# Spreading the context branch over sixteen experts: order edges on TensorE, a deferred expert half, four split buffers

## The chip, the cores and the metric

The kernel runs on one core of one Trainium2 chip. The metric is device microseconds of one execution, as the median of the runs shown. TensorE (PE) multiplies matrices, VectorE (DVE), ScalarE (ACT) and GpSimd (POOL) work on tiles, SyncE (SP) only issues transfers. POOL issues transfers too, from its own queue. The five run in parallel, each through its own list of instructions in order, and wait for one another by semaphores.

## The reference

Two blocks of two layers each over 256 tokens x of width 1024, with a context of 256 tokens beside them in each block; all in float32.

```python
def first_block(x, c, ctx, ...):
    for l in range(2):
        # modulation: mod = silu(c) @ w_ada[l] + b_ada[l]: shifts, scales and gates
        # mLSTM mixer over x, its states started from the context
        x = x + gt1 * (mix_x @ w_out[l])
        # 16 experts, each takes its 32 best tokens
        x = x + gt2 * expert_choice_ffn(modulated_rmsnorm(x, ...), w_router[l], w_e_gate[l], w_e_up[l], w_e_down[l])
    return _rms(x, g_final)

def expert_choice_ffn(xn, w_router, w_gate, w_up, w_down):
    aff = softmax(xn @ w_router); gate, idx = top_k(aff.T, 32); xs = xn[idx]
    hid = silu(einsum('ecd,edf->ecf', xs, w_gate)) * einsum('ecd,edf->ecf', xs, w_up)
    return zeros.at[idx].add(einsum('ecf,efd->ecd', hid, w_down) * gate)

def second_block(x, c, ctx, ...):
    # layer 0: Hyena mixer, of x AND of the second context ctx_2; layer 1: attention of x over both
    ...

def hyena_mixer(h, ...):
    proj = h @ w_in                      # 1024 -> 4 x 2048: x0, x1, v, z
    x0, x1, v = split(short_conv(proj[:, :6144]))
    u = x1 * v
    y = irfft(rfft(u, 512) * rfft(k, 512))[:256] + u * d      # k from a small network
    return (y * x0 * silu(z)) @ w_out
```

The second block's context depends on nothing of the first block. So its Hyena layer can run while the first block's last experts do.

## The kernel before

The program is written with a tile framework: pools hand out buffers by tag (with a number of buffers each), and a scheduler sets each engine's order when the program is built, from the order of the code, a simulated time line and the buffers; at run time that order is fixed.

The stretch that the change touches, in order of time:

- **Layer 1's mLSTM mixer** (`mixer`). A part of the modulation (`ada`: loads of `w_ada` or `ada_w_2`, tag `W`, and matmuls of line 191 into `pad`) is stepped through beside other work. `PLACES` says which part goes where: "M1" and "L1" are in the mixer, ahead of and in the mLSTM core, "R1" is in the router. Parts a1, b0, b1 (second block, 16 loads of one MiB) stand in R1. Behind the core comes the output projection of x (lines 109 to 111 with `mhi`, `mlo`), with four loads of `w_out`.
- **The router** (`route_tokens`): norm, logits, top-k, gathering of the tokens into XS.
- **Layer 1's experts** (`experts`, `expert_k`), only for x (`ns == 1`). An expert has 24 steps of line 823: eight each for gate, up (both on XS) and down (on the transposed hidden tile `hT`). A step is four matmuls of 256 columns, side by side on four column groups; the trace has two records for each float32 matmul. Two steps share a weight tile of one MiB. Six first tiles have buffers of their own (`W2`), all others the ring `W` of five, filled from SP's queue.
- **The context's Hyena layer** (`hyena` with `G == 1`), written behind the experts in the code but placed between them by the scheduler. It has 16 pieces of 128 channels (`ct`). A piece has four projections (`projT`: in two halves; each half splits 128x512 weights into a high part `hi`, line 104 on ACT, and a rest `lo`, line 105 on DVE, two buffers each, and issues 12 matmuls, lines 109 to 111 on `hyx`), then `uf` (line 1058 on POOL), its transposes (line 1059), a forward transform with `fe` (line 1017), the product with the filter `Kt`, and the transform back with `fi` (line 1017, four matmuls of 256 columns). Four pieces form a block, which ends in an output projection (`out_proj`, `projN_steps`: steps of six 512-column matmuls on `hmh`, `hml`). Its weights go through a ring `Wb` of two on POOL's queue. Piece 15 is kept back for the last expert: its loads stand on SP's queue behind a gate on expert 14's hidden tile (`self.late[14]`).
- **The end**: `between` makes the second block's input from x, and the latent Hyena layer begins.

Of the kernel before, what the change touches and what calls it, by code (L numbers as in the profile page):

```python
# [13 lines left out]
OP = mybir.AluOpType  # L14
# [7 lines left out]


SB = 4
SA = 3
AB = dict(atp=2, aP=2, aq=3, atk=2)
HB = dict(Yf=1, Y=1, ht1=1)
PLACES = dict(P0="", M0="01 02 10", L0="", R0="a0", W1="", P1="11", M1="12", L1="", R1="a1 b0 b1")
EVERY = dict(P0=3, L0=1, P1=3, L1=1)


class K:
    def __init__(self, ctx, tc, A, out):
# [12 lines left out]
        self.sbufs = 2  # L46
        self.filler = None
        self.side, self.turn = (None, 1), 0
        self.wgate, self.late = [], {}

    def T(self, shape, tag, bufs=1, dt=F32):
# [55 lines left out]
    def mm3(self, out, l, r, start, stop):  # L107
        mm = self.nc.tensor.matmul
        mm(out, lhsT=l[0], rhs=r[0], start=start, stop=False)  # L109
        mm(out, lhsT=l[0], rhs=r[1], start=False, stop=False)  # L110
        mm(out, lhsT=l[1], rhs=r[0], start=False, stop=stop)  # L111

    def rsqrt(self, out, in_, scale):
# [184 lines left out]
    def projN_steps(self, wts, x, tts, n, pss, start=True, stop=True):  # L298
        nk = x[0].shape[1]
        for k in range(nk):  # L300
            hi = self.T([128, n], "hi", self.sbufs, F32R)
            lo = self.T([128, n], "lo", self.sbufs, F32R)
            self.split(wts(k), hi, lo)
            for q, tt in enumerate(tts):
                c = slice(tt * 128, tt * 128 + 128)
                self.mm3(pss[q], (x[0][:, k, c], x[1][:, k, c]), (hi, lo), start and k == 0, stop and k == nk - 1)
            self.fill()
            yield
# [510 lines left out]
    def expert_k(self, ps, w, k, l, M, N, ns):  # L819

        wt = self.ew(w, k, self.nc.sync.dma_start, ns)
        for j, v in enumerate(l):
            self.nc.tensor.matmul(ps[M * j:M * j + M], lhsT=v, rhs=wt[:, j * N:(j + 1) * N], start=(k == 0), stop=(k == 7))  # L823

    def experts(self, l, xs, F2, XS, SgT, R, early, beside=None):
        nc, A, T = self.nc, self.A, self.T
# [8 lines left out]
        nS = N // 128  # L835
        Y = {}
        for e in range(16):
            q, r = divmod(e, 4)
            pgu = []
# [14 lines left out]
            nc.vector.tensor_tensor(hv, hv, pgu[1], op=OP.mult)  # L854
            pt = self.PT([128, nS, 128])
            for i in range(nS):
                nc.tensor.transpose(pt[:, i], hv[:, i * 128:(i + 1) * 128], self.ident)
            hT = T([128, 4, 128], "hT", 2)
            self.copy(hT[:, :nS], pt)
            py = self.P([128, N])  # L860
            for k in range(8):
                j, i = divmod(k, nS)
                self.expert_k(py, A["w_e_down"][l, e], k, [hT[:, i, M * j:M * j + M]] * G, M, N, ns)
            if r == 0:
                Y = {s: T([128, 1024], "Y", ns) for s, _ in xs}
            for i, (s, x) in enumerate(xs):
                for jj in range(G):
                    p0, c = M * jj + 32 * i, slice(jj * N, (jj + 1) * N)
                    nc.vector.tensor_tensor(Y[s][32 * r:32 * r + 32, c], py[p0:p0 + 32], gt[s][p0:p0 + 32, c], op=OP.mult)  # L869
            if r == 3:  # L870
                for s, x in xs:
                    for t in range(2):
                        for n in range(2):
                            ps = self.PS([128, 512])
                            nc.tensor.matmul(ps, lhsT=SgT[s][:, q, t * 128:(t + 1) * 128], rhs=Y[s][:, n * 512:(n + 1) * 512],  # L875
                                             start=True, stop=True)
                            xv = x[:, t, n * 512:(n + 1) * 512]
                            nc.vector.tensor_tensor(xv, xv, ps, op=OP.add)

        if beside is not None:  # L880
# [102 lines left out]
    def hy_consts(self, three):  # L983
# [9 lines left out]
        dma(fi, A["fi"].rearrange("p (k n) -> p k n", k=4))  # L993
        self.fds, self.fis = (fe,), (fi,)
# [26 lines left out]
    def hyena(self, x, X, gt, dma, blocks, G, three, gate=None):  # L1021
# [3 lines left out]
        for g0, wg in blocks:  # L1025
            m = self.parts([128, blocks[0][1], 256], "hm", 1, True)
            for g in range(g0 // G, (g0 + wg) // G):
# [4 lines left out]
                u = self.parts([128, 2, n], "u", 2, three)  # L1032
                x0s = T([128, G, 256], "x0s", G)
                for i in range(G):
                    ct = G * g + i
                    cv = {}
                    for q, kind in enumerate((1, 2, 0, 3)):
# [7 lines left out]
                        if kind < 3:  # L1045
# [6 lines left out]
                            if kind == 2:  # L1052
                                nc.vector.tensor_tensor(cv[1], cv[1], cv[2], op=OP.mult)

                                pt = self.PT([128, 2, 128])
                                uf = T([128, 2, 128], "uf", 2)
                                for c, op in enumerate((OP.add, OP.subtract)):
                                    nc.gpsimd.tensor_tensor(uf[:, c], cv[1][:, :128], cv[1][:, 128:][:, ::-1], op=op)
                                    nc.tensor.transpose(pt[:, c], uf[:, c], self.ident)
                                self.put([v[:, :, i * 128:(i + 1) * 128] for v in u], pt)  # L1060
                        else:
                            sg = T([128, 256], "cvz", G)
                            nc.scalar.activation(sg, ps, AF.Silu)
                            nc.vector.tensor_tensor(x0s[:, i], sg, cv[0], op=OP.mult)
                pu = []
                pu2 = self.PS([128, 2, 2, n]) if G == 1 else None
                for c in range(2):
# [3 lines left out]
                    pu.append(ps)  # L1071
                Yf = T([128, 2, 2, n], "Yf", HB["Yf"] if three else 1)
                t1 = T([128, 2, n], "ht1", HB["ht1"] if three else 1)
# [8 lines left out]
                py = self.PT([128, G, 256])  # L1082
                for i in range(G):
                    for q in range(4):
                        c, f = divmod(q, 2)
                        self.mmx(py[:, i], [v[:, c, f, i * 128:(i + 1) * 128] for v in Y], [v[:, q] for v in self.fis], q == 0, q == 3)
                i0 = G * g - g0
                nc.vector.tensor_tensor(x0s, x0s, py, op=OP.mult)
                self.split(x0s, m[0][:, i0:i0 + G], m[1][:, i0:i0 + G])
            self.out_proj(x, A["hy_w_out_2"][0], m, g0, wg, gt, dma, wg - G if three and g0 + wg == 16 else 0)  # L1090

# [240 lines left out]
    def run(self):  # L1332
# [7 lines left out]
        if True:  # L1340
# [47 lines left out]
            if True:  # L1388
                with self.psum("ps1", mm=2, tp=1, sm=1):
# [3 lines left out]
                    with self.psum("ps2", "right", mm=2, tp=1, sm=1), self.pool("bga"):  # L1393
                        self.wtag, self.wbufs = "Wb", 2
                        c2 = self.load_x("ctx_2", "hc")
                        self.hy_consts(False)
                        a0 = self.modA(b0[1], 1, self.colv["ng", 0], "a1")
                        gtc = self.row_bcast(b0[0][:, 0], 0, 64, 1, "gtc", 1)
                        X2 = self.modulated(c2, a0, b0[1][:, 0], 1)
                        with self.pool("bgb") as p:  # L1400
                            self.route = dict(self.route, rtmp=p)
                            self.rbufs = 1
                            self.hyena(c2, X2, gtc, pool, [(0, 4), (4, 4), (8, 4), (12, 3)], 1, False)
                            keep, ps2 = (self.cur, self.route), self.ps
# [4 lines left out]
                            X = (T([128, 8, 256], "hyl0", 1, F32R), T([128, 8, 256], "hyl1", 1, F32R))  # L1409
                            self.between(x, X, b0)  # L1410
                            (self.cur, self.route), self.ps = keep, ps2
                            self.hyena(c2, X2, gtc, sync, [(15, 1)], 1, False, self.late[14])
# [189 lines left out]
```

## Time and profile before

| | us |
|---|---|
| median of 3 runs | 2360.59 (2359.33 to 2368.23) |
| the profiled execution | 2366.99 |
| its span | 2365.2 |

| share of the span | |
|---|---|
| TensorE busy | 90% |
| DVE / ACT / POOL busy | 53% / 31% / 8% |
| chain that ended last: PE / DVE / issue / DMA / ACT | 72% / 9% / 8% / 7% / 3% |

The page's averages mix stages with different limits, so the table by stage is the view to read first: busy time of each engine in a stretch, the granted TensorE clock (1.00 is 2.4 GHz, 0.50 is 1.2 GHz), the mean busy share of the core's 16 DMA engines (a stretch that is full reads 1.01 or 1.02), and GB/s. Matmuls are pipelined: a later one starts before an earlier one ends, so the time that one takes up is read from start to start.

### The profile page before, as it was taken

The numbers are of one execution on the slowest core, as the hardware profiler recorded it, in microseconds if no ns is written. First come the engines' busy times: TensorE is split into PE (matmuls) and PEld (weight loads), VectorE is DVE, ScalarE is ACT, GpSimd is POOL, SyncE is SP. The second block draws the span as 40 slices with busy tenths as digits, with TensorE's granted clock in tenths as the row PEclk, the third lists the DMA queues.
The fourth block names the chain that finished last, engine by engine and source line by source line (L and its number), as shares of the span: only waits on it lengthen the run. The fifth ranks groups of instructions, "written<-read, shape, count | busy, mean of one in ns | idle before, by whom it ended". The sixth has DMA issues, their size and how long they took to land.

```text
span 2365.2 us, 35049 instructions
## 1 busy us (share of the span) xinstructions
PE 2135.7 (90%) x13966; PEld 1436.1 (61%) x13966; DVE 1250.4 (53%) x2533; ACT 737.5 (31%) x1414; POOL 187.7 (8%) x315
## 2 busy tenths in 40 slices
PE   5999988999999989998799998898777999999998
PEld 3776664343343436864376766665234999979786
DVE  3954444333433337654355555544125878875776
ACT  3323331000000014343233222222013555555665
POOL 1000000011010100000011011100001110100100
PEclk8999999999999999999899999998777999999999
DMA  8247545999999996459799999988996545435320
GB/s 342 99 157 312 204 184 193 413 415 415 414 413 415 414 405 251 137 194 370 295 351 365 372 374 370 351 336 327 421 421 262 185 144 188 168 132 189 126 81 26
DMA packets 129588, 664.09 MB, mean 281 GB/s; under 512 B 12666, under 2 KB 23429, under 8 KB 62352
## 3 DMA queue, kind: packets, MB, share of 16 engines
q1 hardware_dynamic: 115616, 602.89, 66.0%
q0 software_dynamic: 13808, 58.96, 6.6%
q8 instruction: 110, 1.80, 0.3%
q14 instruction: 54, 0.44, 0.1%
HBM read 656.56 MB, written 5.24 MB: 280 GB/s over the span
## 4 chain that ended last, share of the span: by engine, by line
PE 72%; DVE 9%; issue 8%; DMA 7%; ACT 3%; POOL 1%; SPq 0%; DVEq 0%; POOLq 0%; ACTq 0%
PE pmm L823 16%; PE pmm L109 12%; PE pmm L111 11%; PE pmm L110 11%; PE pad L191 3%; PE psm L875 2%; DMA W<-in_w_e_gate 1%; DVE lo L105 1%; DMA W<-in_w_e_up 1%; PE ptp L1017 1%; DMA W<-in_w_ada 1%; PE pmm L798 1%; PE pad L978 1%; DMA W<-in_ada_w 1%; PE ppo L1247 1%
## 5 line engine op out<-in xcount | busy, mean ns | idle before, releaser
L823 PE MATMUL pmm<-W,XS 128*32 128x256 f32 (+1 forms) x3040 | 378.8, 478 | 39.7 <-DMA W<-in_w_e_gate 20.3
L105 DVE TENSOR_TENSOR lo<-W,hi 128x512 fp32r<-128x512 f32 (+1 forms) x420 | 283.7, 680 | 187.1 <-ACT hi L104 184.2
L104 ACT CAST hi<-W 128x512 fp32r<-128x512 f32 (+1 forms) x420 | 255.5, 612 | 352.0 <-PE pmm L110 162.9
L823 PEld LDWEIGHTS pmm<-W,XS 128*32 128x32 f32 (+1 forms) x3040 | 127.0, 123 | 241.3 <-issue 151.1
L823 PE MATMUL pmm<-W,hT 128*32 128x256 f32 (+1 forms) x1536 | 190.1, 483 | 20.2 <-DVE hT L101 8.3
L111 PE MATMUL pmm<-hyx,lo 128*128 128x256 f32 x640 | 191.6, 299 | 10.6 <-DVE lo L105 10.6
L109 PE MATMUL pmm<-hyx,hi 128*128 128x256 f32 x640 | 193.4, 302 | 4.8 <-ACT hi L104 4.8
L110 PE MATMUL pmm<-hyx,hi 128*128 128x256 f32 x640 | 185.8, 290 | 0.0
L105 DVE TENSOR_TENSOR lo<-Wb,hi 128x512 fp32r<-128x512 f32 x160 | 109.4, 692 | 117.3 <-ACT hi L104 116.3
L104 ACT CAST hi<-Wb 128x512 fp32r<-128x512 f32 x160 | 96.8, 619 | 209.4 <-PE pmm L110 138.3
L869 DVE TENSOR_TENSOR Y<-pmm,gt 32x512 f32<-32x512 f32 (+1 forms) x128 | 70.9, 554 | 143.5 <-PE pmm L823 141.8
L109 PE MATMUL pmm<-hyl,hi 128*128 128x256 f32 x512 | 144.5, 283 | 1.7 <-DVE rtmp L697 1.7
L110 PE MATMUL pmm<-hyl,hi 128*128 128x256 f32 x512 | 144.1, 282 | 0.0
L111 PE MATMUL pmm<-hyl,lo 128*128 128x256 f32 x512 | 143.1, 283 | 0.0
L109 PEld LDWEIGHTS pmm<-hyx,hi 128*128 128x128 f32 x640 | 126.6, 198 | 23.7 <-ACT hi L104 16.6
L111 PEld LDWEIGHTS pmm<-hyx,lo 128*128 128x128 f32 x640 | 126.3, 197 | 22.3 <-DVE lo L105 14.1
L823 PEld LDWEIGHTS pmm<-W,hT 128*32 128x32 f32 (+1 forms) x1536 | 65.6, 125 | 117.6 <-issue 68.6
L110 PEld LDWEIGHTS pmm<-hyx,hi 128*128 128x128 f32 x640 | 126.6, 198 | 2.4 <-issue 2.2
L851 ACT ACTIVATE h<-pmm 128x256 f32<-128x256 f32 (+1 forms) x31 | 15.1, 488 | 362.1 <-PE pmm L823 361.9
L191 PE MATMUL pad<-W,cpad 128*32 128x512 f32 x576 | 91.0, 643 | 21.6 <-DMA W<-in_w_ada 16.7
L854 DVE TENSOR_TENSOR h<-h,pmm 128x512 f32<-128x512 f32 (+1 forms) x32 | 17.7, 552 | 171.9 <-ACT h L851 89.5
L109 PEld LDWEIGHTS pmm<-hyl,hi 128*128 128x128 f32 x512 | 97.4, 190 | 3.4 <-issue 1.9
(516 smaller groups left out, 4084.1 us busy)
## 6 DMA issues: line engine op xcount, KB each, us to landing
W<-in_w_e_gate SPq DMA_DIRECT2D x128, 1024.0 KB, 11.2
W<-in_w_e_up SPq DMA_DIRECT2D x128, 1024.0 KB, 11.2
W<-in_w_e_down SPq DMA_DIRECT2D x128, 1024.0 KB, 11.2
W<-in_w_ada SPq DMA_DIRECT2D x48, 1024.0 KB, 6.6
W<-in_hyw SPq DMA_DIRECT2D x32, 1024.0 KB, 5.1
Wb<-in_hyw POOLq DMA_DIRECT2D x30, 1024.0 KB, 8.9
W<-in_ada_w SPq DMA_DIRECT2D x24, 1024.0 KB, 5.2
W<-in_at_w_in SPq DMA_DIRECT2D x16, 1024.0 KB, 5.0
```

The source lines that it names most:

```text
L104: self.nc.scalar.copy(hi, w)
L105: self.nc.vector.tensor_tensor(lo, w, hi.bitcast(F32), op=OP.subtract)
L109: mm(out, lhsT=l[0], rhs=r[0], start=start, stop=False)
L110: mm(out, lhsT=l[0], rhs=r[1], start=False, stop=False)
L111: mm(out, lhsT=l[1], rhs=r[0], start=False, stop=stop)
L191: nc.tensor.matmul(ps[32 * j:32 * j + 32, :], lhsT=self.cpad[:, blk, k0 + k, :], rhs=wt[:, k, j * 512:(j + 1) * 512], start=(k0 + k == 0), ...
L798: nc.tensor.matmul(ps, lhsT=v, rhs=S[s][:, t], start=(t == 0 and q == 0), stop=(t == 1 and q == 1))
L823: self.nc.tensor.matmul(ps[M * j:M * j + M], lhsT=v, rhs=wt[:, j * N:(j + 1) * N], start=(k == 0), stop=(k == 7))
L869: nc.vector.tensor_tensor(Y[s][32 * r:32 * r + 32, c], py[p0:p0 + 32], gt[s][p0:p0 + 32, c], op=OP.mult)
L875: nc.tensor.matmul(ps, lhsT=SgT[s][:, q, t * 128:(t + 1) * 128], rhs=Y[s][:, n * 512:(n + 1) * 512], start=True, stop=True)
L978: nc.tensor.matmul(ps[:, i, f], lhsT=self.fd[:, t, i * 256 + f * 128:i * 256 + (f + 1) * 128], rhs=ab[:, i, t], start=(t == 0), stop=(t == 1))
L1017: self.nc.tensor.matmul(out, lhsT=l[0], rhs=r[0], start=start, stop=stop)
```

## The change

1. **Order edges.** `mm3` returns its first matmul. While `mixed` is set (the first 15 pieces of the context layer), every step of `projT` and `projN_steps` calls `place`: step j may not stand on TensorE's list ahead of the pair of expert steps number 1.2 j - 4. The edge orders only; no semaphore comes of it.
2. **Deferred halves.** In layer 1 an expert's second half (transposes, down, Y) is issued behind the gate and up of the next one. In the context layer, `pend` keeps the back transform and the output projection until `uf` of the next piece has been issued, and the transposes of `uf` are issued one projection later than before.
3. **Four split buffers** `hi` and `lo` for the context layer in place of two (`sbufs`), and two of `Yf`.
4. **Folded back transform.** `fi` is loaded with half its columns; four matmuls of 128 columns give an even and an odd part, and a copy, an addition and a subtraction (reversed) give the two halves. The forward transform was folded already.
5. **PLACES.** Parts a1, b0, b1 of the modulation move from R1 to L1.

Two things stay as they are for x's own Hyena layer (`three`): `flush` is called at once, and its transforms are not folded.

```diff
+SHARE, LEAD = 1.2, 4
-PLACES = dict(P0="", M0="01 02 10", L0="", R0="a0", W1="", P1="11", M1="12", L1="", R1="a1 b0 b1")
+PLACES = dict(P0="", M0="01 02 10", L0="", R0="a0", W1="", P1="11", M1="12", L1="a1 b0 b1", R1="")
...
+    def place(self, first):
+
+        if self.mixed is None:
+            return
+        i = int(self.mixed * SHARE) - LEAD
+        self.mixed += 1
+        if 0 <= i < len(self.clusters):
+            self.tc.add_manual_dep(first.ins, self.clusters[i].ins.name,
+                                   mybir.DependencyInfo(mybir.DependencyClass.NoSync, mybir.DependencyReason.DATA),
+                                   reason="share")
...
-                self.mm3(ps, (hi[:, k], lo[:, k]), (x[0][:, kk, c0:c0 + n], x[1][:, kk, c0:c0 + n]), kk == 0, kk == 7)
+                first = self.mm3(ps, (hi[:, k], lo[:, k]), (x[0][:, kk, c0:c0 + n], x[1][:, kk, c0:c0 + n]), kk == 0, kk == 7)
+                if k == 0:
+                    self.place(first)
...
-            self.nc.tensor.matmul(ps[M * j:M * j + M], lhsT=v, rhs=wt[:, j * N:(j + 1) * N], start=(k == 0), stop=(k == 7))
+            last = self.nc.tensor.matmul(ps[M * j:M * j + M], lhsT=v, rhs=wt[:, j * N:(j + 1) * N], start=(k == 0), stop=(k == 7))
+        if ns == 1 and k % 2:
+            self.clusters.append(last)
...
+            if put_off and e:
+                down(e - 1, last)
+            last = hv
+            if not put_off:
+                down(e, hv)
+        if put_off:
+            down(15, last)
...
-            fe, fi = T([128, 2, 256], "fe"), T([128, 4, 256], "fi")
+            fe, fi = T([128, 2, 256], "fe"), T([128, 4, 128], "fi")
...
-                                    nc.tensor.transpose(pt[:, c], uf[:, c], self.ident)
-                                self.put([v[:, :, i * 128:(i + 1) * 128] for v in u], pt)
+                                if not three:
+                                    self.flush()
...
+                        if q == (1 if three else 2):
+                            pt = self.PT([128, 2, 128])
+                            for c in range(2):
+                                nc.tensor.transpose(pt[:, c], uf[:, c], self.ident)
+                            self.put([v[:, :, i * 128:(i + 1) * 128] for v in u], pt)
...
+                self.pend.append(lambda Y=Y, x0s=x0s, m=m, i0=G * g - g0: self.back(Y, x0s, m, i0, blocks[0][1]))
+                if three:
+                    self.flush()
+            self.pend.append(lambda m=m, g0=g0, wg=wg: self.out_proj(x, A["hy_w_out_2"][0], m, g0, wg, gt, dma,
+                                                                     wg - G if three and g0 + wg == 16 else 0))
+            if three:
+                self.flush()
+        self.flush()
+
+    def flush(self):
+
+        p, self.pend = self.pend, []
+        for f in p:
+            f()
+
+    def back(self, Y, x0s, m, i0, width):
+
+        G = x0s.shape[1]
+        if not m:
+            m += self.parts([128, width, 256], "hm", 1, True)
+        py = self.PT([128, G, 256])
+        if len(Y) == 1:
+
+            for c in range(2):
+                for f in range(2):
+                    self.mmx(py[:, 0, c * 128:(c + 1) * 128], [v[:, c, f] for v in Y], [v[:, 2 * c + f] for v in self.fis],
+                             f == 0, f == 1)
+            y = self.T([128, 2, 128], "yh", 1)
+            ye = self.T([128, 128], "ye", 1)
+            nc = self.nc
+            nc.scalar.copy(ye, py[:, 0, :128])
+            nc.vector.tensor_tensor(y[:, 0], ye, py[:, 0, 128:], op=OP.add)
+            nc.vector.tensor_tensor(y[:, 1], ye[:, ::-1], py[:, 0, 128:][:, ::-1], op=OP.subtract)
+            y = y.rearrange("p a b -> p (a b)")[:, None]
...
+                        self.sbufs = 4
...
+                            self.mixed = 0
                             self.hyena(c2, X2, gtc, pool, [(0, 4), (4, 4), (8, 4), (12, 3)], 1, False)
+                            self.mixed = None
```

How this moves the instructions, at three places. In the names, a letter tag stands before the arrow for the tile written and behind it for those read; lines of the changed program are some 15 to 70 further down (823 becomes 842, 109 becomes 112, 186 becomes 201, 320 becomes 339, 895 becomes 926).

First, TensorE where the context's first fifteen pieces are done, before: expert 11, alone.

```order
L823 MATMUL pmm<-W,XS_7295 32x256 x8
L823 MATMUL pmm<-W,XS_7296 32x256 x16
L823 MATMUL pmm<-W,XS_7295 32x256 x16
L823 MATMUL pmm<-W,XS_7296 32x256 x16
L857 MATMUL ptp<-cf,h_8983 128x128 x2
L823 MATMUL pmm<-W,hT 32x256 x32
L875 MATMUL psm<-Y,SgT 128x512
```

Now, TensorE at the end of gate and up of expert 14 and the start of the down half of expert 13 behind it.

```order
L842 MATMUL pmm<-W,XS_7295 32x256 x8
L842 MATMUL pmm<-W,XS_7296 32x256 x8
L112 MATMUL pmm<-hi,hmh 128x512
L113 MATMUL pmm<-lo,hmh 128x512
L114 MATMUL pmm<-hi,hml 128x512
L842 MATMUL pmm<-W,XS_7296 32x256 x8
L112 MATMUL pmm<-hi,hmh 128x512
L113 MATMUL pmm<-lo,hmh 128x512
L114 MATMUL pmm<-hi,hml 128x512
L864 MATMUL ptp<-cf,h_9348 128x128 x2
L842 MATMUL pmm<-W,hT 32x256 x8
```

Context steps (here of the output projection of pieces 12 to 14) now stand between the pairs of expert steps until expert 14, where before experts 11 to 14 had none between them.

Second, SP's queue ahead of layer 1's experts, before: the modulation's `ada_w` behind the mixer's `w_out`.

```order
L186 DMA W<-in_w_ada 128x2048 x8
L320 DMA W<-in_w_out 128x4x512 x4
L186 DMA W<-in_ada_w 128x2x1024 x4
L186 DMA W<-in_ada_w 128x2048 x8
L186 DMA W<-in_ada_w 128x2x1024 x4
L895 DMA W<-in_w_e_up 128x2048
```

Now, the same place.

```order
L201 DMA W<-in_w_ada 128x2048 x8
L201 DMA W<-in_ada_w 128x2x1024 x4
L201 DMA W<-in_ada_w 128x2048 x8
L201 DMA W<-in_ada_w 128x2x1024 x4
L339 DMA W<-in_w_out 128x4x512 x4
L926 DMA W<-in_w_e_up 128x2048 x2
```

The sixteen loads of a1, b0 and b1 have moved ahead of the four of the output projection.

Third, POOL's queue in the context layer, before.

```order
L1042 DMA Wb<-in_hyw 128x2048
L1058 TENSOR_TENSOR uf<-cv_9720 128x128 x2
L1042 DMA Wb<-in_hyw 128x2048
L1030 DMA Kt<-Kd 128x512
L1042 DMA Wb<-in_hyw 128x2048
L1058 TENSOR_TENSOR uf<-cv_9904 128x128 x2
```

Now, the same place.

```order
L1073 DMA Wb<-in_hyw 128x2048 x2
L1088 TENSOR_TENSOR uf<-cv_9718 128x128 x2
L1061 DMA Kt<-Kd 128x512
L1073 DMA Wb<-in_hyw 128x2048 x2
L1088 TENSOR_TENSOR uf<-cv_9894 128x128 x2
```

Each `uf` now stands behind both weight loads of the next piece, where it stood behind one.

## Rows read from the trace of the kernel before

**Rows 1.** The page's head: span and number of instructions.

```profile
span 2365.2 us, 35049 instructions
```

**Rows 2.** Table by stage: busy us (xcount) of PE, PEld, DVE, ACT, POOL, clock, DMA share, GB/s.

```profile
1020.00:1049.00 29.00, 25.89 (x173) 21.23 (x172) 18.85 (x73) 16.06 (x51) 0.48 (x2) 1.00 0.32 118
1049.00:1101.00 52.00, 50.44 (x236) 27.07 (x236) 21.13 (x41) 15.00 (x28) 2.82 (x4) 0.93 0.77 282
...
1190.00:1640.00 450.00, 411.06 (x3694) 305.71 (x3693) 240.47 (x477) 130.04 (x251) 45.36 (x79) 0.97 0.92 355
1640.00:1756.00 116.00, 78.04 (x808) 29.55 (x806) 14.78 (x30) 2.28 (x6) 0.30 (x2) 0.75 1.00 412
...
1148.00:1786.00 638.00, 543.04 (x4986) 369.86 (x4982) 280.97 (x557) 151.38 (x294) 51.25 (x91) 0.91 0.94 371
...
1330.00:1470.00 140.00, 128.32 (x1205) 96.53 (x1204) 75.61 (x152) 42.35 (x82) 15.64 (x27) 1.00 0.96 373
```

**Rows 3.** TensorE's waits from 1190 to 1640: total us, times, longest; ten rows.

```profile
PE pmm L111 <- DVE lo L105: 10.6, 11, 1.7
PE ptp L1059 <- POOL uf L1058: 7.1, 9, 1.4
...
PE pmm L109 <- ACT hi L104: 4.6, 7, 1.5
...
PE pmm L823 <- DVE hT L101: 1.0, 2, 0.5
```

**Rows 4.** TensorE's groups from 1190 to 1640: count, busy us, mean ns, idle before.

```profile
L111 PE MATMUL pmm<-hyx,lo 128*128 128x256 f32 x475 | 142.8, 301 | 10.6 <-DVE lo L105 10.6
...
L823 PE MATMUL pmm<-W,XS 128*32 128x256 f32 x1152 | 75.9, 385 | 0.0
L823 PE MATMUL pmm<-W,hT 128*32 128x256 f32 x640 | 41.2, 384 | 3.1 <-ACT hT L99 2.1 <-DVE hT L101 1.0
...
L109 PE MATMUL pmm<-hi,hmh 128*128 128x512 f32 x58 | 21.3, 444 | 1.9 <-ACT hi L104 1.9
...
L1059 PE MATMUL ptp<-cf,uf 128*128 128x128 f32 x30 | 9.1, 308 | 7.7 <-POOL uf L1058 7.1
```

**Rows 5.** TensorE in order of time, around 1320: start, us, engine, line, operation.

```profile
1316.66 1.07 PE L823 MATMUL pmm<-W,XS 128*32 128x256 f32 x16
...
1317.88 0.28 PE L109 MATMUL pmm<-hyx,hi 128*128 128x256 f32 x1
1318.00 0.28 PE L110 MATMUL pmm<-hyx,hi 128*128 128x256 f32 x1
...
1323.20 1.05 PE L1017 MATMUL psm<-u,fe 128*128 128x128 f32 x8
...
1326.05 1.99 PE L1017 MATMUL ptp<-fi,Yf 128*128 128x256 f32 x8
1327.69 0.47 PE L109 MATMUL pmm<-hyx,hi 128*128 128x256 f32 x1
```

**Rows 6.** The first layer's experts, layer 1's experts alone, and there TensorE's longest wait.

```profile
440.00:860.00 420.00, 392.98 (x1932) 162.18 (x1930) 139.78 (x235) 17.15 (x29) 40.82 (x76) 1.00 1.01 414
...
1700.00:1750.00 50.00, 32.18 (x324) 11.61 (x324) 2.95 (x7) 1.14 (x3) 0.30 (x2) 0.70 1.01 421
...
PE pmm L823 <- DMA W<-in_w_e_up: 15.1, 14, 2.8
```

**Rows 7.** SP's queue and TensorE in order of time, and line 191 alone by stretch.

```profile
1013.18 6.03 SPq L320 DMA_DIRECT2D W<-in_w_out  x4
1044.47 54.33 SPq L186 DMA_DIRECT2D W<-in_ada_w  x16
...
1049.32 2.51 PE L191 MATMUL pad<-W,cpad 128*32 128x512 f32 x8 [2.68 <-DMA W<-in_ada_w]
1052.91 0.79 PE L109 MATMUL pmm<-hi,mhi 128*128 128x512 f32 x1 [0.46 <-ACT mhi L635]
...
1049.00:1101.00 52.00, 16.76 (x96) 2.77 (x96) 0.93 0.77 282
```

More of the change, by code (lines that the diff above doesn't have):

```diff
@@ L48, in __init__ @@
         self.side, self.turn = (None, 1), 0
+        self.mixed, self.clusters = None, []
         self.wgate, self.late = [], {}
+        self.pend = []
     def T(self, shape, tag, bufs=1, dt=F32):
@@ L108, in mm3 @@
         mm = self.nc.tensor.matmul
-        mm(out, lhsT=l[0], rhs=r[0], start=start, stop=False)
+        first = mm(out, lhsT=l[0], rhs=r[0], start=start, stop=False)
         mm(out, lhsT=l[0], rhs=r[1], start=False, stop=False)
         mm(out, lhsT=l[1], rhs=r[0], start=False, stop=stop)
+        return first
+    def place(self, first):
[7 more added lines that the diff above has]
+                                   reason="share")
     def rsqrt(self, out, in_, scale):
@@ L305, in projN_steps @@
                 c = slice(tt * 128, tt * 128 + 128)
-                self.mm3(pss[q], (x[0][:, k, c], x[1][:, k, c]), (hi, lo), start and k == 0, stop and k == nk - 1)
+                first = self.mm3(pss[q], (x[0][:, k, c], x[1][:, k, c]), (hi, lo), start and k == 0, stop and k == nk - 1)
+                if q == 0:
+                    self.place(first)
             self.fill()
@@ L836, in experts, with down @@
         Y = {}
+        put_off = ns == 1
+        def down(e, hv):
+            q, r = divmod(e, 4)
+            pt = self.PT([128, nS, 128])
+            for i in range(nS):
+                nc.tensor.transpose(pt[:, i], hv[:, i * 128:(i + 1) * 128], self.ident)
+            hT = T([128, 4, 128], "hT", 2)
+            self.copy(hT[:, :nS], pt)
+            py = self.P([128, N])
+            for k in range(8):
+                j, i = divmod(k, nS)
+                self.expert_k(py, A["w_e_down"][l, e], k, [hT[:, i, M * j:M * j + M]] * G, M, N, ns)
+            if r == 0:
+                Y.update({s: T([128, 1024], "Y", ns) for s, _ in xs})
+            for i, (s, x) in enumerate(xs):
+                for jj in range(G):
+                    p0, c = M * jj + 32 * i, slice(jj * N, (jj + 1) * N)
+                    nc.vector.tensor_tensor(Y[s][32 * r:32 * r + 32, c], py[p0:p0 + 32], gt[s][p0:p0 + 32, c], op=OP.mult)
+            if r == 3:
+                for s, x in xs:
+                    for t in range(2):
+                        for n in range(2):
+                            ps = self.PS([128, 512])
+                            nc.tensor.matmul(ps, lhsT=SgT[s][:, q, t * 128:(t + 1) * 128], rhs=Y[s][:, n * 512:(n + 1) * 512],
+                                             start=True, stop=True)
+                            xv = x[:, t, n * 512:(n + 1) * 512]
+                            nc.vector.tensor_tensor(xv, xv, ps, op=OP.add)
         for e in range(16):
-            q, r = divmod(e, 4)
             pgu = []
@@ L854, in experts @@
             nc.vector.tensor_tensor(hv, hv, pgu[1], op=OP.mult)
[L855 to L878, printed above, removed]
+            if put_off and e:
[5 more added lines that the diff above has]
+            down(15, last)
         if beside is not None:
@@ L1025, in hyena @@
         for g0, wg in blocks:
-            m = self.parts([128, blocks[0][1], 256], "hm", 1, True)
+            m = []
             for g in range(g0 // G, (g0 + wg) // G):
@@ L1032, in hyena @@
                 u = self.parts([128, 2, n], "u", 2, three)
-                x0s = T([128, G, 256], "x0s", G)
+                x0s = T([128, G, 256], "x0s", 2)
                 for i in range(G):
@@ L1071, in hyena @@
                     pu.append(ps)
-                Yf = T([128, 2, 2, n], "Yf", HB["Yf"] if three else 1)
+                Yf = T([128, 2, 2, n], "Yf", HB["Yf"] if three else 2)
                 t1 = T([128, 2, n], "ht1", HB["ht1"] if three else 1)
@@ L1081, in hyena @@
                     self.split(Yf, *Y)
[L1082 to L1089, printed above, removed]
@@ new lines, in hyena @@
+            if three:
[22 more added lines that the diff above has]
+            y = y.rearrange("p a b -> p (a b)")[:, None]
+        else:
+            for i in range(G):
+                for q in range(4):
+                    c, f = divmod(q, 2)
+                    self.mmx(py[:, i], [v[:, c, f, i * 128:(i + 1) * 128] for v in Y], [v[:, q] for v in self.fis], q == 0, q == 3)
+            y = py
+        self.nc.vector.tensor_tensor(x0s, x0s, y, op=OP.mult)
+        self.split(x0s, *[v[:, i0:i0 + G] for v in m])
```

6 lines of the change are left out of this document (3 added, 3 removed).

## The prediction

> **What bounds the kernel now.** I read the table by stage first [rows 2], then the waits of TensorE in the longest stage [rows 3], then its groups and the spacing of single matmuls [rows 4, 5]. The sum is made against the profiled execution: span 2365.2 us [rows 1], 1.8 us around it, 2367.0 in all. That is 6.4 us above the median of the three runs, 2360.6, so a gain is taken from 2367.0 and carried over to the median.
>
> The change acts between about 1020 and 1815 us; what follows (the latent Hyena and the attention) keeps its order. In that stretch three things are to be seen. From 1190 to 1640 the second layer's experts and the context branch share TensorE. It is 411 us of 450 busy at a granted clock of 0.97, while the DMA engines are at 0.92 and not at 1.01 [rows 2]. None of the ten waits listed for TensorE there is for a weight load; they sum to 38.2 us, 21 of them in three rows for the `hi` and `lo` pieces, of which the largest and the smallest stand, and 7.1 for `uf` [rows 3]. So this stage is bound by TensorE and its split chain, and the loads wait for free `W` buffers. From 1640 to 1756 the context branch has run out of work: the experts stand alone, DMA is at its ceiling (1.00, 412 GB/s), TensorE has only 78 us of work in 116 and its clock is 0.75 [rows 2]; now it does wait for expert loads [rows 6]. One resource is short in the first stage and another in the second, so moving context work from the first into the second can pay. The third thing: from 1020 to 1049 DMA is at 0.32 [rows 2], because four `w_out` tiles issued at 1013 hold the `W` ring until the projection begins at 1052.9, and the sixteen `ada_w` loads behind them start only at 1044.47 [rows 7].
>
> **The change, part by part.**
>
> *The three modulation pieces (a1, b0, b1) move from the router into the mLSTM core* (`PLACES`). Sixteen loads and sixteen groups of L191 move ahead of the output projection on TensorE, and on SP ahead of its four loads. What goes: 96 records, 12 groups, 16.8 us of TensorE between 1049 and 1101, in the middle of the projection that x waits for [rows 7]; the other four stand where the norm is awaited and go for little. What comes: sixteen groups in the core, about 1.0 us each at full clock, 16 us, where TensorE is already 26 us of 29 busy [rows 2]. By work alone that is a draw. The loads are the doubt. At the 421 GB/s of the experts' stage [rows 6] one MiB takes 2.49 us, so sixteen take 40 us from 1013.2, until 1053, and the first `w_out` tile follows at 1056, against a projection that now begins at 1052.9. Best case: the 2.68 us wait of the first load [rows 7], the slow clock around 1050 (0.93 for the stretch) and the router's last groups go, 8 us gained. Worst: the ring goes round four times and each round pays such a wait, 4 x 2.7 = 11 us lost. I take **3 us gained**, near the draw.
>
> *The stage of experts and context.* Its end is set by whichever of two sums is longer.
>
> DMA: from the restart at 1148 to the last expert load at about 1786 the engines work 638 x 0.94 = 600 us [rows 2]. The bytes stay the same but for a quarter MiB of `fi`. At a share of 1.01 that is 594 us, so **44 us is all that better filling can give**.
>
> TensorE, at full clock: a pair of expert steps (16 records) takes 1.0 us, 1.2 with the switch to the other kind of matmul and back (1316.66 to 1317.88, against 0.12 between context matmuls at 1317.88 and 1318.00) [rows 5]. A context step of 12 matmuls takes 12 x 0.12 = 1.43 us, and an output step of six 512-column matmuls about the same. The table of groups gives 1792 records, 112 pairs; 1424 `hyx` matmuls, 119 steps; 174 `hm` matmuls, 29 steps; 15 blocks [rows 4]. A block's transforms and transposes cost about 3.2 us: 1.05 forward, 1.64 back (1326.05 to 1327.69) [rows 5] and the rest switches. So 112 x 1.2 + 148 x 1.43 + 15 x 3.2 = 394; with some 11 for Y and the hidden transposes, and the 38 us of waits, 443. The stage took 450, so the prices hold.
>
> After the change a block lies against one expert: 10 steps to 12 pairs, since an order edge holds step j behind pair 1.2 j - 4. Per expert TensorE then needs 12 x 1.2 + 10 x 1.43 + 2.3 (folded back transform about 1.05, as the forward one) + 0.9 = 31.9 us. DMA needs 12 x 2.49 = 29.9 for the experts plus 2.75 MiB of context. The context's price comes from the mixed stage: 450 x 0.92 / 1.01 = 410 us, less 112 x 2.49 = 279, is 131 us for 15 x 2.75 MiB, 3.2 us each. So 29.9 + 8.8 = 38.7 us. **DMA becomes the bound, with TensorE at 82% of it.** The saved waits (four split buffers: up to 21 us; `uf` awaited half a block later: 7; the hidden transpose awaited one expert later: 3) and the smaller back transform (16 x 0.6 = 10 us) are worth nothing added to that. They are the slack that keeps TensorE under the loads. Their own cost is an ACT copy and three small DVE operations a block, on engines that are 130 and 240 us of 450 busy [rows 2].
>
> How full does DMA get? The first layer's experts show it: from 440 to 860 DMA is at 1.01 while TensorE is 393 us of 420 busy at a clock of 1.00 [rows 6]. Against that, the ring here is five tiles, and the context starts late and then catches up: about 29 steps within 18 pairs, TensorE 72 us against 73 of DMA, so every wait counts. I leave 4 us there (a share of 0.96, the best that the mixed stage reaches now [rows 2]), 6 in the remaining eleven experts (0.995 over 426 us), and 4 in the last expert, whose 30 us hold the last context block and now 16 rather than 12 pairs after the first load. 44 - 14 = **30 us gained**.
>
> On the queues: `uf` now stands on POOL behind both loads of the next block, and `Kt` behind it. Those loads wait for buffers that the splits free four steps ahead, so I cost it at nothing; without that cover, up to the 7.1 us of today's `uf` waits. On SP the last block's two loads again stand behind the gate of expert 14, with five expert loads ahead of them: nothing.
>
> Sum: 2367.0 - 3 - 30 = 2334.0, which on the median is 2360.6 - 33 = **2328 us**.
>
> **Rivals.**
>
> *The memory already gives what it can.* If 355 GB/s [rows 2] were the ceiling of this mixture, filling would gain nothing and only the 3 us remain: 2357. Against it stand 421 GB/s with experts alone [rows 6] and a share of 0.92. The Trainium skill ("DMA: Bandwidth & Descriptors", section "Where 436 GB/s comes from") says that the HBM side, about 358 GB/s per core, binds a load into SBUF. By that rule the 237 MB of the stage need 661 us and the change gains nothing. This trace differs, with its 421, and I go by the trace. Chance 0.08.
>
> *The order edges only spread the same stall.* TensorE runs in order; each context step stands behind an expert pair that waits for its load, and a late context tile holds the experts. Then the share stays at today's best, 0.96 [rows 2]: 600 / 0.96 = 625, 13 us gained, 2345. For it: a five-tile ring. Against it: none of today's waits is for a load. Chance 0.20.
>
> *The modulation loads starve the core.* 8 us lost instead of 3 gained: 2339. Chance 0.14.
>
> *Slower: the clock falls.* With experts alone TensorE stops for every load, and its clock is 0.70 between 1700 and 1750 [rows 6]. The changed order puts such a stop into every pair. Needing 31.9 us at full clock, TensorE is the bound again once its mean clock is under 31.9 / 38.7 = 0.82, and the gain is gone at 0.77 (31.9 / 0.77 = 41.4, 2.7 us more for each of eleven experts). At 0.70 an expert takes 45.6, 76 us more in all: 2403. The Trainium skill ("TensorE: Matmul & The Clock Gate", section "HAM oscillation — how this bites in real kernels") describes this for a kernel whose every burst ends in a wait for its load; by it the time would be this rival's. The stage of experts alone agrees with the page. The first layer's experts speak against it here: their loads too fill DMA, at 1.01, but other work (the filter kernels) lies between them on TensorE, and the clock is at 1.00, which is 2.4 GHz [rows 6]. The new mixture has context steps between all its loads. Chance 0.06.
>
> **How the numbers follow.** The forecast has 0.52. 0.5% is 11.8 us, about what a measurement of this kernel tells from no change: 2349 to 2372. Faster: 0.52 + 0.14 + 0.12 of the 0.20 (its centre is only 4 us inside) = 0.78; same: 0.08 + 0.08 = 0.16; slower: 0.06. The range runs from all 44 + 8 us gained, 2309, to 2353, past the second rival; outside it lie the ceiling and the clock, 0.14.
>
> **What would show it.** Right: no stretch of experts alone; a DMA share of 0.99 or more in most of the stage; TensorE's waits there for expert loads, not for `lo` or `uf`; a granted clock above 0.85; the stage of experts and context ending near 1753 rather than 1786. The `W` ring should be busy between 1020 and 1049, and the projection's end (1101) at 1093 to 1100. Wrong: `lo` waits in the catch-up, a clock near 0.75, or L191 waiting for `ada_w` in the core. What would overturn it most is a price for context bytes that rises when they lie beside every expert, since the 3.2 us a MiB is worked out from one mixture.

## The result and the profile after

The changed kernel takes 2322.9 us, median of four runs (2320.6 to 2324.8), beside 2362.5 us for the kernel before: a ratio of 0.983, 95% interval 0.981 to 0.985. That is 39.6 us less. The forecast was 2328, inside 2309 to 2353. A later set of runs gave 2323.0 us and 0.9826 (0.9812 to 0.9840).

The page's head, and the table by stage of the trace after (busy us and count of PE, PEld, DVE, ACT, POOL, then clock, DMA share and GB/s):

```profile
span 2322.0 us, 35052 instructions
```

```profile
1020.00:1049.00 29.00, 28.83 (x187) 17.64 (x188) 14.29 (x55) 11.38 (x34) 0.00 (x0) 1.00 0.76 273
1049.00:1101.00 52.00, 48.43 (x237) 29.32 (x233) 23.77 (x59) 17.83 (x43) 3.30 (x5) 0.93 0.75 285
1101.00:1148.00 47.00, 31.31 (x160) 21.51 (x160) 25.45 (x60) 14.74 (x24) 0.90 (x2) 0.82 0.46 179
1148.00:1190.00 42.00, 31.49 (x338) 15.52 (x335) 11.87 (x22) 13.10 (x24) 5.87 (x10) 0.80 0.88 360
1190.00:1640.00 450.00, 402.59 (x3888) 281.88 (x3888) 229.22 (x471) 120.89 (x241) 39.52 (x74) 0.97 1.00 405
1640.00:1743.00 103.00, 89.33 (x893) 60.06 (x891) 51.47 (x105) 22.00 (x45) 4.14 (x9) 0.96 1.00 392
1148.00:1743.00 595.00, 523.40 (x5114) 357.46 (x5110) 292.57 (x597) 155.98 (x310) 49.53 (x93) 0.96 0.99 399
```

The span is 43.2 us shorter than in [rows 1]. In the same 450 us from 1190 on the DMA engines now move 405 GB/s where they moved 355 [rows 2], with TensorE no busier (403 us for 411). The stretch of experts alone, where TensorE had 78 us of work in 116 and a clock of 0.75, is gone: until 1743 TensorE is 89 us busy of 103 at 0.96. Before 1148 the gain is not there: DMA is busier from 1020 to 1049 (0.76 for 0.32), but from 1101 to 1148 it is less busy than it was, 0.46 for 0.67, and by 1148 the bytes are the same (31 MB from 1020 on). The row of before:

```profile
1101.00:1148.00 47.00, 35.42 (x253) 19.89 (x257) 23.07 (x59) 12.98 (x20) 2.41 (x5) 0.85 0.67 274
```

TensorE's waits from 1190 to 1640 (total us, times, longest):

```profile
PE ptp L1098 <- POOL uf L1088: 10.7, 6, 4.1
PE pmm L842 <- DMA W<-in_w_e_up: 9.5, 8, 2.0
PE pmm L842 <- DMA W<-in_w_e_gate: 8.7, 8, 2.1
PE ptp L1048 <- DVE Yf L1112: 5.0, 4, 3.5
...
PE pmm L113 <- DVE lo L108: 0.9, 1, 0.9
```

Beside [rows 3] the `lo` and `hi` waits have gone from 21 us to 0.9, and TensorE now waits for expert loads, which it did not do there. The wait for `uf` has grown from 7.1 to 10.7.

Where the 43.2 us are, by the first expert step and the last of the matmuls that add the experts' result to x. First the first step of before, then of after (count, min/median/max ns, first and last start), then the last matmuls of after:

```profile
L823 PE MATMUL pmm<-W,XS x256: 376/379/637, 1140.4 to 1184.3; 128*32 128x256 f32 x128
```

```profile
L842 PE MATMUL pmm<-W,XS x288: 379/379/637, 1145.7 to 1198.6; 128*32 128x256 f32 x144
...
L882 PE MATMUL psm<-Y,SgT x8: 1061/1140/1222, 1749.4 to 1759.0; 128*128 128x512 f32 x8
```

The experts start 5.3 us later (1145.7 for 1140.4). The last of those matmuls started at 1802.2 before, so the stage of experts and context takes 613.3 us where it took 661.8: 48.5 less. 48.5 - 5.3 = 43.2, all of the difference between these two traces.

### The profile page after: what moved, and what is told of

Its sections match the earlier page's. It is cut to its first block, busy times and chain, and to the rows that moved or that the text cites. A ratio compares the mean times of both kernels' runs of the same rounds, so it can differ in the third digit from the quotient of the medians.

```text
span 2322.0 us, 35052 instructions
## 1 busy us (share of the span) xinstructions
PE 2112.0 (91%) x13966; PEld 1422.8 (61%) x13966; DVE 1257.3 (54%) x2565; ACT 741.9 (32%) x1430; POOL 184.1 (8%) x315
## 5 line engine op out<-in xcount | busy, mean ns | idle before, releaser
L842 PE MATMUL pmm<-W,XS 128*32 128x256 f32 (+1 forms) x3040 | 372.3, 466 | 29.3 <-DMA W<-in_w_e_up 18.0
L842 PE MATMUL pmm<-W,hT 128*32 128x256 f32 (+1 forms) x1536 | 189.5, 470 | 19.8 <-DMA W<-in_w_e_down 10.7
L114 PE MATMUL pmm<-hyx,lo 128*128 128x256 f32 x640 | 183.6, 288 | 2.6 <-DVE lo L108 2.6
L206 PE MATMUL pad<-W,cpad 128*32 128x512 f32 x576 | 90.6, 640 | 17.7 <-DMA W<-in_w_ada 16.8
L112 PEld LDWEIGHTS pmm<-hyl,hi 128*128 128x128 f32 x512 | 97.4, 190 | 3.4 <-issue 1.9
L113 PEld LDWEIGHTS pmm<-hyl,hi 128*128 128x128 f32 x512 | 97.3, 190 | 0.0
```

What stands on the lines that cost most here:

```text
L112: first = mm(out, lhsT=l[0], rhs=r[0], start=start, stop=False)
L206: nc.tensor.matmul(ps[32 * j:32 * j + 32, :], lhsT=self.cpad[:, blk, k0 + k, :], rhs=wt[:, k, j * 512:(j + 1) * 512], start=(k0 + k == 0), ...
L842: last = self.nc.tensor.matmul(ps[M * j:M * j + M], lhsT=v, rhs=wt[:, j * N:(j + 1) * N], start=(k == 0), stop=(k == 7))
```

## Experiments

Three readings were open. **A:** the order edges fill the DMA engines, and the rest of the change is slack under the loads. **B:** the stage was bound by TensorE and became faster because waits and work went (four split buffers, deferral, folding). And of the modulation pieces: does their move cost the 5.3 us, or is it a draw?

**The edges away.** Only the line that starts the counting is left out:

```diff
-                            self.mixed = 0
                             self.hyena(c2, X2, gtc, pool, [(0, 4), (4, 4), (8, 4), (12, 3)], 1, False)
```

> The changed kernel without the order edges: on TensorE's list the context steps of the first 15 pieces then stand within experts 1 to 9.3 (as before: 1 to 10.5), and five experts have none between them. Theory A (spreading fills the DMA engines, and that is the gain): most of the gain is lost, 2350 to 2360, and a stretch of experts alone is back. Theory B (the gain is the 38 us of waits and the 10 us of the folded transform, gone from a stage that TensorE bounds; with both gone, 9.3 experts and the context need 394 us of TensorE, from 1146 to 1540, and 6.7 experts at 29.9 us end at 1740, where the changed kernel ends too): within 5 us of the changed kernel, 2318 to 2328.

2369.1 us; ratio to before 1.001 (1.000 to 1.003). Without its edges the change gives nothing at all. The table by stage, and TensorE's waits from 1590 to 1740, show the old picture again, earlier:

```profile
1190.00:1590.00 400.00, 370.99 (x3380) 283.36 (x3372) 235.23 (x491) 127.27 (x262) 43.59 (x78) 0.98 0.93 352
...
1640.00:1690.00 50.00, 33.63 (x320) 11.32 (x312) 5.33 (x12) 1.14 (x3) 0.00 (x0) 0.71 1.01 421
```

```profile
PE pmm L842 <- DMA W<-in_w_e_up: 19.9, 20, 2.4
PE pmm L842 <- DMA W<-in_w_e_down: 14.4, 15, 1.6
PE pmm L842 <- DMA W<-in_w_e_gate: 11.8, 13, 1.6
```

The cheaper context work does end some 50 us sooner (1590 for 1640), but with fewer experts beside it, and the time comes back as a longer stretch of experts alone, at a clock of 0.71 and with 46 us of waits for loads in 150. Theory B falls. The 394 us that it counted from 1146 on were wrong too: until 1190 the context's steps had hardly begun, so those 44 us hold little of its work.

**The edges alone**, put into the kernel before (two split buffers, no deferral, no folding, old PLACES): `mm3` returns its first matmul, every step calls `place`, `expert_k` fills `clusters`, and

```diff
+                            self.mixed = 0
                             self.hyena(c2, X2, gtc, pool, [(0, 4), (4, 4), (8, 4), (12, 3)], 1, False)
+                            self.mixed = None
```

> The kernel before with the order edges alone (mm3 returns its first matmul, clusters, place): two split buffers, no deferral, the unfolded back transform, the modulation pieces in the router. Per expert TensorE then needs 12 x 1.2 + 10 x 1.43 + 3.2 + 0.9 = 32.8 us and some 2.5 us of today's waits, 35.3, still under the loads. Theory A (the edges are the change, all else is slack): 2318 to 2330. Theory C (the edges need the buffers and the deferral, since a context step that waits now holds an expert step whose load is due): 2340 or more.

2318.2 us, ratio 0.980 (0.978 to 0.982): the whole gain, from one of the five edits.

```profile
1190.00:1640.00 450.00, 410.79 (x3899) 284.23 (x3898) 224.05 (x443) 119.44 (x230) 42.76 (x74) 0.98 0.99 402
1640.00:1743.00 103.00, 92.19 (x909) 61.92 (x908) 51.80 (x102) 23.41 (x46) 5.30 (x11) 0.97 1.01 412
```

TensorE is as busy as before (411 us of 450), with the same operations a piece and the same buffers; only which step lies beside which load has changed, and the loads go from 355 to 402 GB/s.

**The other parts, undone one at a time in the changed kernel.** Two split buffers (`self.sbufs = 4` becomes 2, twice), the down half at once, and the context layer's own order:

```diff
-        put_off = ns == 1
+        put_off = False
```

```diff
-                        if q == (1 if three else 2):
+                        if q == 1:
...
-                if three:
-                    self.flush()
+                self.flush()
```

> The changed kernel with two split buffers for the context layer instead of four; on TensorE's list the spread stays (ten context steps an expert from expert 4 on). Theory A (loads bound the stage, the buffers are slack): 2323 to 2328. Theory B (the waits for the lo and hi pieces were the loss): up to the 21 us of those waits come back, about 2344.

> The changed kernel with an expert's down half issued at once instead of behind the next expert's gate and up. Both theories: the wait for the transposed hidden tile comes back, 3 us in the stage before. Theory A: hidden under the loads, 2323 to 2326. Theory B: 2326 to 2328.

> The changed kernel with the context layer's own order as before: the transposes of uf right behind it, the back transform and the output projection issued at once; the edges, buffers, folding and the experts' deferred half stay. The trace of after has 14.6 us of waits of TensorE for uf although its transposes come one projection later. Theory A (slack under the loads): 2320 to 2328. Theory B (these waits count): uf is awaited at once by each of 15 pieces, 2330 to 2345.

Measured, as ratio to before: 0.982 (0.980 to 0.983), 0.983 (0.982 to 0.985) and 0.981 (0.979 to 0.983), with medians of 2323.9, 2329.4 and 2321.9 us. Each interval overlaps that of the changed kernel (0.9812 to 0.9840). The waits do come back. With two split buffers, and with the context's own order, they cost nothing that can be measured. TensorE from 1190 to 1740, with two buffers, then with the down half at once:

```profile
PE pmm L842 <- DMA W<-in_w_e_up: 12.3, 8, 2.4
PE pmm L842 <- DMA W<-in_w_e_down: 7.1, 5, 3.5
PE pmm L112 <- ACT hi L107: 5.8, 7, 1.0
PE pmm L114 <- DVE lo L108: 5.5, 6, 3.0
```

```profile
PE ptp L864 <- DVE h L903: 15.2, 11, 2.1
```

Only with the down half at once are the loads a little behind (391 GB/s from 1190 to 1640); its median lies 6 us higher, above what either theory expected, and the interval neither shows nor excludes such a cost. Edges alone have the down half at once too, at 2318.2 us. The folded back transform was not undone by itself; the run with edges alone has it unfolded.

**Who bounds the stage now?** One run takes a third of the context's split matmuls away (in `mm3`, one of three products while `mixed` is set), another takes half of the projections' weight loads away (the context's result is then not the layer's):

```diff
+        if self.mixed is not None:
+            mm(out, lhsT=l[1], rhs=r[0], start=False, stop=stop)
+            return first
```

```diff
-                        if q % 2 == 0:
+                        if q % 2 == 0 and (q == 0 or self.mixed is None):
                             wt = self.W([128, 2, 8, 128])
```

> The changed kernel with one of the three products of every split matmul of the first 15 context pieces left out (the one of the weight's high part and the input's rest, or of the first operand's high part and the second's rest), so the context's result is less exact; bytes and buffers stay. TensorE needs about 4.8 us less in each of 13 experts. Theory A (loads bound the stage): within 5 us of the changed kernel, 2318 to 2326. Theory B (TensorE still has a part in it): 20 to 50 us faster.

> The changed kernel with one weight load of 1 MiB for a context piece instead of two (projections 3 and 4 use the tile of 1 and 2 again, so the context's result is not the layer's); TensorE's work is kept. 15 MiB less. Theory A (loads bound the stage, a context MiB costs what an expert MiB does, 2.49 us): 37 us faster, about 2286. By the 3.2 us a MiB of the prediction: 48 us faster, 2275, as far as TensorE lets it. Theory B (TensorE bounds): no change, 2318 to 2328.

Less TensorE work: 2308.9 us, 14 less for an estimated 62 us of work, between the ranges of the two theories. Fewer loads: 2288.3 us, 34.6 less for 15 MiB, 2.3 us a MiB. So it is the loads that bound most of the stage, but not all of it, and the 2.3 us are a lower bound for what a MiB of loads takes: from 1190 to 1290 DMA moved only 349 GB/s in that run. The table by stage shows where TensorE had a part, the changed kernel first, then with less TensorE work:

```profile
1190.00:1290.00 100.00, 93.82 (x900) 73.81 (x899) 61.30 (x133) 34.87 (x71) 11.89 (x23) 1.00 0.99 389
1290.00:1390.00 100.00, 89.91 (x882) 60.99 (x886) 49.38 (x101) 25.44 (x51) 7.18 (x14) 0.97 0.98 401
1390.00:1490.00 100.00, 85.96 (x829) 56.47 (x818) 47.17 (x93) 23.34 (x45) 8.44 (x15) 0.98 1.01 418
```

```profile
1190.00:1290.00 100.00, 82.12 (x764) 58.79 (x765) 62.74 (x137) 33.12 (x70) 13.00 (x25) 0.97 0.99 397
1290.00:1390.00 100.00, 81.36 (x787) 49.35 (x786) 46.69 (x94) 25.59 (x52) 7.69 (x15) 0.92 1.01 420
```

389 and 401 GB/s in the first 200 us, while the context catches up, against 418 behind it: that is the largest place that was left.

**A slower catch-up.** The edges at pair 1.12 j + 6, with the context's own order and the old PLACES; and, in the kernel before, edges alone at 1.1 j + 8:

```diff
-SHARE, LEAD = 1.2, 4
+SHARE, LEAD = 1.12, -6
```

> The changed kernel with the modulation pieces and the context layer's own order as before, and the edges at pair 1.12 j + 6 instead of 1.2 j - 4, so that the context's steps catch up over more of experts 1 to 3 (from 1190 to 1290 DMA is at 0.96 to 0.98 in the runs with edges, at 1.01 later). Theory A (what is left of the gain lies in that catch-up): 4 us less than edges alone, about 2313. Otherwise, if the piece behind it runs late at the end: 2318 or more.

> The kernel before with the order edges alone, at pair 1.1 j + 8. Theory A, as for the run before this one: about 2314; if the start was not what held it, 2318.

The first took 2305.5 us (2303.9 to 2307.4), ratio 0.975 (0.974 to 0.976): 18 us better than the changed kernel, and faster than edges alone. From 1190 to 1290, TensorE's groups of the changed kernel, then of this one (count, busy us, mean ns, idle before), and this one's row of the stage:

```profile
L842 PE MATMUL pmm<-W,XS 128*32 128x256 f32 x256 | 17.1, 385 | 0.0
L842 PE MATMUL pmm<-W,hT 128*32 128x256 f32 x128 | 8.6, 385 | 0.0
```

```profile
L842 PE MATMUL pmm<-W,XS 128*32 128x256 f32 x352 | 23.5, 385 | 1.6 <-DMA W<-in_w_e_up 1.1 <-DMA W<-in_w_e_gate 0.4
L842 PE MATMUL pmm<-W,hT 128*32 128x256 f32 x128 | 8.6, 385 | 0.0
```

```profile
1190.00:1290.00 100.00, 95.68 (x925) 69.17 (x924) 58.04 (x121) 32.23 (x65) 10.62 (x21) 1.00 1.01 406
```

30 pairs of expert steps in that stretch instead of 24 (480 and 384 records of 16 to a pair), and 406 GB/s instead of 389. The second run missed: 2327.8 us, ratio 0.985 (0.983 to 0.986), ten us above edges alone. In its stretch from 1190 to 1290 the catch-up hardly changed (26 pairs, 25 with edges alone) and DMA moved 354 GB/s, where edges alone moved 373:

```profile
1190.00:1290.00 100.00, 92.86 (x867) 69.60 (x866) 51.91 (x108) 30.14 (x60) 11.98 (x20) 0.98 0.92 354
```

At 11 steps an expert, with unfolded transforms and 2.5 us of waits, TensorE would need, an expert, 14.4 + 11 x 1.43 + 3.2 + 0.9 + 2.5 = 36.7 us against about 37 of loads (an estimate from the prices above), so it has no slack left. That this is why it lost, and not another effect of the new order, was not shown. Nor was it fully separated which of the first run's differences its 18 us need: they come with three edits together. But the changed kernel with nothing but the old PLACES took 2316.1 us in the same set of runs (below), and in its trace the stretch reads:

```profile
1190.00:1290.00 100.00, 93.18 (x882) 72.57 (x881) 61.23 (x132) 33.17 (x68) 12.57 (x25) 0.99 0.97 371
```

So some 11 of the 18 us are left for the later start and the context's own order, which alone gave 1. From 371 to 406 GB/s in 100 us is 3.5 MB, by an estimate 8 us at 418 GB/s, so the slower catch-up is probably most of the 11.

**The modulation pieces back in the router.** One line, run twice, the second time beside the changed kernel itself:

```diff
-PLACES = dict(P0="", M0="01 02 10", L0="", R0="a0", W1="", P1="11", M1="12", L1="a1 b0 b1", R1="")
+PLACES = dict(P0="", M0="01 02 10", L0="", R0="a0", W1="", P1="11", M1="12", L1="", R1="a1 b0 b1")
```

> The changed kernel with the three modulation pieces a1, b0, b1 back in the router (PLACES as before), all else kept. The trace of after has the first expert step at 1145.7 us against 1140.4 before. Theory A (the move costs what the traces show): about 5 us faster than the changed kernel, 2318. Theory B (the move was a small gain, as predicted, and the 5 us come from elsewhere, for instance from loads that the new order lets start earlier): 3 us slower, 2326.

> The changed kernel itself once more, beside the next one on the same chip. Theory A (the modulation pieces' move costs 3 to 5 us): 3 to 5 us slower than the next kernel. Theory D (the move is a draw by work, and the later start of the experts in the trace of after is not its doing): within 1.5 us of it.

> The changed kernel with the modulation pieces back in the router, for the comparison with the one before it. Theory A: about 2318. Theory D: the same time as the changed kernel.

Back in the router: 2319.7 us, ratio 0.980 (0.978 to 0.981), then 2316.1 us, 0.979 (0.977 to 0.981); the changed kernel beside the second: 2323.0, 0.983 (0.981 to 0.984). Each time the intervals just touch, and each time the changed kernel is some 3 to 7 us slower. In the traces the first expert step stands at 1138.5 to 1144.2 us in the six with the old PLACES (mean 1140.7) and at 1143.0 to 1145.7 in the eight with the new ones (mean 1144.2). That is 3.5 us on the mean, and the two traces of the kernel with the pieces back in the router already lie 5.7 apart, so the 5.3 us of one pair of traces are not exact. The move is not a gain; most likely it costs 3 to 7 us. The trace after shows how (SP's queue, then TensorE in order of time):

```profile
1013.77 48.02 SPq L201 DMA_DIRECT2D W<-in_ada_w  x16
1062.28 9.05 SPq L339 DMA_DIRECT2D W<-in_w_out  x4
```

```profile
1065.57 5.34 PE L206 MATMUL pad<-W,cpad 128*32 128x512 f32 x24 [0.61 <-DVE adbC L215]
...
1075.08 0.70 PE L112 MATMUL pmm<-hi,mhi 128*128 128x512 f32 x2
```

The output projection begins at 1075.1 instead of 1052.9 [rows 7], 22.2 us later, and from there to the first expert step it takes 70.6 us instead of 87.5: 16.9 saved. 22.2 - 16.9 = 5.3. What the modulation's matmuls take of TensorE ahead of the projection, before (line 191) and after (line 206):

```profile
1010.00:1054.00 44.00, 6.34 (x40) 0.85 (x32) 0.96 0.47 171
```

```profile
1010.00:1076.00 66.00, 27.89 (x160) 5.60 (x160) 1.00 0.90 340
```

120 more records, 15 groups of eight, for 21.6 us: 1.4 us a group.

## Why the prediction was right, step by step

- **What bounds the kernel: right.** TensorE in the mixture, loads in the stretch behind it, and moving work from the one to the other pays. The run without edges and the run with nothing but edges show it from both sides.
- **The size of the stage's gain: too small.** 30 us were forecast, of 44 "that better filling can give"; 48.5 came. The step that failed is the ceiling, 638 x 0.94 = 600 us of DMA work, and with it the 3.2 us a MiB for the context. Both take the busy share for work done. By bytes, 638 us at 371 GB/s are 237 MB, and at 421 GB/s [rows 6] that is 562 us (an estimate), 76 less. In the trace of after the mixture itself moves 418 GB/s from 1390 to 1490 at a share of 1.01, where before it moved 373 at 0.96 [rows 2]; and 15 MiB of context loads taken away were worth 2.3 us each, a lower bound that shows nothing of 3.2 but does not exclude it by itself; the bytes do. The prediction named this price as its weakest point, though it feared the other direction. The Trainium skill ("Perfetto Trace Analysis", section "Identifying the Most-Contended Engine") says to judge DMA by the bytes moved and not by how long its engines are occupied; this trace agrees, with a share of 0.96 that still had 12% to give.
- **How full it gets: right by the share, too full by the bytes.** 14 us were left unfilled in the forecast. By bytes it is more: 595 us for 237 MB, 33 above the 562, with the start (360 GB/s from 1148 to 1190), the catch-up (389 and 401) and the end (392) its largest parts. The slower catch-up brought 18 us, together with the old PLACES and the context's own order.
- **The slack: right.** Split buffers, deferral and folding were costed at nothing added to the sum, and undone one by one (folding only within edges alone) they change nothing that can be measured, except that up to 6 us for the expert's deferred half are not excluded. In the sum, a block's 2.3 us should be 3.2 - 0.6 = 2.6; with it TensorE needs 32.2 us an expert, still far below the 38.7 of the loads.
- **`uf` behind two loads on POOL: cover thinner than thought.** Costed at nothing, with 7.1 us as the price without cover; its waits are 10.7 us up to 1640 and 14.6 up to 1740. With the context's own order they stay (14.9 us up to 1740), and with two split buffers they are 3.5, and the kernel's time is the same both times; so they seem to cost little, though no run removed them alone.
- **The modulation pieces: wrong sign, inside the bounds.** 3 us gained were forecast and 5.3 lost in the traces. What goes was about right: 16.8 us forecast, and 16.9 less from the projection to the first expert step. What comes was taken at 1.0 us a group, 16 in all, and came to 22.2: the twelve groups of [rows 7] already said 16.8 / 12 = 1.4 us each, and 16 x 1.4 is 22.4. The last matmul of the projection starts at 1108.7, where 1093 to 1100 was given as a sign of being right. The starvation of the core did not come; TensorE waited there for no `ada_w` load.
- **The rivals.** The memory ceiling of 355 GB/s is out: the mixture moves 418. The Trainium skill's figure that the prediction cites for it ("DMA: Bandwidth & Descriptors", section "Where 436 GB/s comes from") is about 358 GB/s from HBM. This trace differs from it, with the 418. A share that stays at 0.96 is out too, since it is 1.00. The falling clock is out: 0.97, though TensorE now stops for loads 20 us of 450. Even with a third of the context's matmuls left out, 50 us of waits for loads in 553 went with a clock of 0.92. Where experts stand alone (edges away), it is 0.71. That TensorE "stops for every load" there was too strong: in the trace of before it waits 28 times for 60 pairs of steps from 1640 to 1800.
- **The sum.** Forecast 3 + 30 = 33, traces 48.5 - 5.3 = 43.2, medians 39.6. Two terms missed, 8 us down and 18 up, and partly made up for each other: that the time came within 5 us of the forecast is in part luck, though its mechanism held.

## What to carry to other kernels

Where two streams of work have different needs (one of loads, one of TensorE), look for a stretch in which the one has run out: spreading it evenly by order alone was worth more here than any buffer or shortened operation, and a saving of the busy engine in the mixture can come back as a longer stretch without it. Judge how much room DMA has by GB/s against the fullest stretch of the same trace, not by its busy share. Where work moves rather than goes, price it at both places from the same kind of row.

## What the runs showed of the hardware

Not expected: a DMA busy share of 0.96 at 373 GB/s [rows 2] and of 1.01 at 418, of the same kinds of loads from the same two queues, if in another proportion. The last twentieth of the share is an eighth of the bytes. And from 1190 to 1740 the granted clock held at 0.92 to 0.97 on the mean, between the levels of 1.2 and 2.4 GHz but near the upper one, in the mixtures of the changed kernel and of the run with less TensorE work. TensorE stopped there for loads again and again (23 and 50 us of waits), with context steps between the stops; where experts stood alone it was 0.70 to 0.77.
